# Hybrid decoder trunk: layer 0's scale weights through five buffers of the first stage's own pool

## The chip, the cores and the metric

One Trainium2 chip, of which one core is used. The metric is the device time of one execution in microseconds (us). PE is TensorE, DVE is VectorE, ACT is ScalarE, POOL is GpSimd, and SP is SyncE, whose queue issues every load spoken of here.

## What is computed

Two layers of a decoder trunk over 256 tokens of width 2048, in float32. Each layer has a token-mixing part (four head groups side by side) and a gated feed-forward part, and both are modulated by six vectors that come from one conditioning vector c. Cut to what matters:

```python
def reference(x, c, ada_w, ada_b, norm_mix, ...):
    cond = jax.nn.silu(c)
    for l in range(DEPTH):
        mod = cond @ ada_w[l] + ada_b[l]                  # 2048 x 12288 weights
        sh1, sc1, g1, sh2, sc2, g2 = [m[:, None, :] for m in jnp.split(mod, 6, axis=-1)]
        h = rms_norm(x, norm_mix[l]) * (1.0 + sc1) + sh1  # this stage, in layer 0
        x = x + g1 * hybrid_mixer(h, w_in[l], ...)        # u = h @ w_in comes first
        h = rms_norm(x, norm_ffn[l]) * (1.0 + sc2) + sh2
        x = x + g2 * conv_glu_ffn(h, ffn_up[l], ...)
    return x
```

The change concerns sh1 (shift) and sc1 (scale) of layer 0, which must be there before the first input projection can begin.

## The kernel before

The width of 2048 is cut into 16 chunks of 128 partitions, `k` = 0 to 15. The activations stand transposed (channels on partitions, 256 tokens in the free dimension). The product of c with the adaLN weights is not made on TensorE: `ada_mul` (line 167) lets VectorE multiply a 128x1024 tile of weights, half a chunk's rows, with `cond` and sum along the row. A vector of six needs two such tiles per chunk, 512 KB each. For most of them this runs beside the matmuls of other stages, through `ada_jobs`. For layer 0's shift and scale there is nothing yet to run beside, so they are made in the first stage itself, `mix_in_behind`, one chunk per turn of its loop. This loop is the stage that the change touches. Its turn for chunk `k` is:

1. two loads of scale weights (`ada_load`, L163), and two multiplies on DVE (L167), then `sc` (L470);
2. a load of `wconv`, 512 KB (`load_w`, L242);
3. two loads of shift weights, two multiplies, then `sh` (L470), and `amul` from `sc` (L474);
4. the chunk's normalised activations: `t` on DVE (L394) and `actw` on ACT (L396). A copy is split in two parts for later (ACT L492, DVE L493, tile `act`);
5. matmuls of `wconv` with the chunk (L415, 8 instructions, which the trace shows as 16 passes), a load of `wlq`, 448 KB, and its matmuls (L415, 5 instructions, 10 passes; L427, 2 instructions, 4 passes).

Each turn so loads five tiles of 512 KB and one of 448 KB, all on the one queue of SP, in this order: scale, scale, `wconv`, shift, shift, `wlq`. SP goes through its queue in order: an issue that waits for its buffer holds all that stand behind it. Two rings of buffers decide these waits. All adaLN weights go through the tag `adaw` of the pool `ap_`, three buffers; the loads of weights for TensorE go through the tag `raw` of the pool `weights`, `RAW` = 4 buffers, so that in this stage `wconv` and `wlq` have two each. A load takes a buffer when the last reader of the tile that was in it is done: a multiply on DVE for `adaw`, matmuls for `raw`. Before the loop come the load of x (2 MB), and the norm's sum of squares (`norm_stats`), which shares DVE with the first multiplies. The tiles of the stage lie in its pool `sp`, which is closed at its end.

After the loop come the convolution group's taps on DVE (L621) beside a matrix product of 16 chunks on PE (L322), and then the rest of the layer. The tag `adaw` serves `ada_jobs` from there on.

```python
            for s, m in ((1, sc), (0, sh)):
                if s == 0:
                    w = load_w(io["wconv"][l, k], True)
                ada_dot(l, s, k, raws[s])
```

Of the kernel before, what the change touches and what calls it, by code (L numbers as in the profile page):

```python
# [11 lines left out]
F32 = mybir.dt.float32  # L12
# [8 lines left out]
P = 128  # L21
T = 256
D = 2048
# [43 lines left out]
GATE = ((1, 0, 0, 1, 1), (1, 0, 0, 1, 1))  # L67
DW_LATE = 800
RAW = 4

JOIN = 8
GAINS = 2 * 4 * 64 + 2 * 96 + 2 * 32
# [3 lines left out]
def tile_trunk(ctx: ExitStack, tc: tile.TileContext, io, out, L):  # L76
    nc = tc.nc

    def pool(stack, name, bufs=1, **kw):
        return stack.enter_context(tc.tile_pool(name=name, bufs=bufs, reuse_waits="tile", **kw))  # L80
# [3 lines left out]
    ap_ = pool(ctx, "ada")  # L84
# [16 lines left out]
    def load_constants():  # L101
        nc.sync.dma_start(con, io["con"])
        msk = wp.tile([P, 1024], F32, tag="raw", name="msk", bufs=RAW)[:, 0:2 * P]
        nc.sync.dma_start(msk, io["msk"])
# [37 lines left out]
    def vec(l, name):  # L142
        o, w = VEC[name]
        if o >= NVEC:
            if (l, 1) not in vecs:
                vecs[l, 1] = cp.tile([P, NVECS], F32, name=f"vs{l}")
                nc.sync.dma_start(vecs[l, 1], io["vecs"][l])
            return vecs[l, 1][:, o - NVEC:o - NVEC + w]
        if (l, 0) not in vecs:
            vecs[l, 0] = cp.tile([P, NVEC], F32, tag="vec", name="vec", bufs=1)  # L150
            nc.sync.dma_start(vecs[l, 0], io["vec"][l])
        return vecs[l, 0][:, o:o + w]
# [4 lines left out]

    dots = []

    def ada_load(l, s, j, hf):  # L160
        w = ap_.tile([P, D // 2], F32, tag="adaw", name="adaw", bufs=3)
        with tc.issue_after(last_load[0].ins) if gate[0] else ExitStack():
            nc.sync.dma_start(w, io["ada"][l, s * KD + j, hf])  # L163
        return w

    def ada_mul(w, s, j, hf, raw):
        nc.vector.scalar_tensor_tensor(  # L167
            w, w, 1.0, cond[:, hf * 1024:hf * 1024 + 1024], op0=ALU.mult, op1=ALU.mult,
            accum_out=raw[:, hf, j:j + 1],
        )  # L170

    def ada_dot(l, s, j, raw):
        for hf in range(2):
            ada_mul(ada_load(l, s, j, hf), s, j, hf, raw)

    def run_dots():
        while dots:
# [60 lines left out]
    def load_w(src, whole=False):  # L238

        n = src.shape[-1]  # L240
        raw = wp.tile([P, 1024], F32, tag="raw", name="raw", bufs=RAW)
        last_load[0] = nc.sync.dma_start(raw[:, :n], src)  # L242
        tick(rate[0])
        if whole:
            return raw, None
        hi = wp.tile([P, 1024], F32R, tag="hi", name="hi", bufs=3)
        nc.scalar.copy(hi[:, :n], raw[:, :n])  # L247
        lo = wp.tile([P, 1024], F32R, tag="lo", name="lo", bufs=3)
        sub = nc.vector.tensor_sub(lo[:, :n], raw[:, :n], hi[:, :n].bitcast(F32))  # L249
        if dots:  # L250

            with tc.high_priority(offset=-late[0]), tc.issue_after(sub.ins):
                run_dots()
        return hi, lo
# [79 lines left out]
    def act_whole():  # L334
        return actp.tile([P, 4, T], F32, tag="act", name="actw", bufs=12)
# [12 lines left out]
    def norm_stats(x, sp, pp, tag):  # L348

        ss = pp.tile([P, 2, T], F32, tag=tag, name="ss")  # L350
        acc = sp.tile([P, 4, T], F32, name="nacc")
        for c in range(4):
            xc = x[:, 4 * c:4 * c + 4, :]
            if c == 0:
                nc.scalar.activation(acc, xc, AF.Square)
                continue
            sq = sp.tile([P, 4, T], F32, tag="nsq4", name="sq", bufs=2)
            nc.scalar.activation(sq, xc, AF.Square)
            nc.vector.tensor_add(acc, acc, sq)
        nc.vector.tensor_add(acc[:, 0:2, :], acc[:, 0:2, :], acc[:, 2:4, :])  # L360
        for c in range(2):
            nc.tensor.matmul(ss[:, 0, :], ones, acc[:, c, :], start=(c == 0), stop=(c == 1))
        r = sp.tile([P, T], F32, tag="nr", name="r", bufs=1)
        rsqrt(r, ss[:, 0, :], D)
        return r
# [25 lines left out]
    def norm_chunk(dst, xc, r, a, sh, sp):  # L391

        t1 = sp.tile([P, T], F32, tag="nsq", name="t1", bufs=2)
        nc.vector.scalar_tensor_tensor(t1, xc, a, r, op0=ALU.mult, op1=ALU.mult)  # L394
        if is_whole(dst):
            nc.scalar.activation(dst, t1, AF.Identity, bias=sh)  # L396
            return
        nc.scalar.activation(dst[:, 0, :], t1, AF.Identity, bias=sh)
        nc.vector.scalar_tensor_tensor(  # L399
            dst[:, 1, :], t1, sh, dst[:, 0, :].bitcast(F32), op0=ALU.add, op1=ALU.subtract  # L400
        )

    def norm_hs():
        hs = []
        for _ in range(KD // 2):
            ht = act_pair()
            hs += [ht[:, 0], ht[:, 1]]
        return hs

    def mm_t(ps, w, h, G, first, last):  # L410

        prods = products(w, h, True)
        for m in range(G):
            for i, (ww, xx) in enumerate(prods):
                nc.tensor.matmul(  # L415
                    ps[m // 2][:, m % 2, :], ww[:, m * P:(m + 1) * P], xx,
                    start=(first and i == 0 and m % 2 == 0), stop=(last and i == len(prods) - 1),
                    skip_group_check=True,
                )

    def mm_n(outs, w, h, first, last):

        prods = products(w, h, False)
        for tt in range(2):
            for i, (ww, xx) in enumerate(prods):
                for o, c0, c1, f in outs(tt):
                    nc.tensor.matmul(  # L427
                        o, xx[:, tt * P:(tt + 1) * P], ww[:, c0:c1],
                        start=(first and i == 0 and f), stop=(last and i == len(prods) - 1),
                        skip_group_check=True,  # L430
                    )
# [19 lines left out]
    def mix_in_behind(l, x, sp, pp, mr, conv):  # L451

        r = norm_stats(x, sp, pp, "gp")
        a = cp.tile([P, KD], F32, tag="amul", name="amul", bufs=2)
        g, ab = vec(l, "norm_mix"), vec(l, "ada_b")
        sh = cp.tile([P, KD], F32, name="sh0")
        sc = cp.tile([P, KD], F32, name="sc0")
        raws = [cp.tile([P, 2, KD], F32, name=f"raw0_{i}") for i in range(2)]
        hs, hw = norm_hs(), []
        for _ in range(KD // 4):  # L460
            t = act_whole()
            hw += [t[:, i, :] for i in range(4)]
        ps = [pp.tile([P, 2, T], F32, tag="gp", name="gt") for _ in range(4)]
        px = [pp.tile([P, 2, T], F32, tag="gx", name="gt") for _ in range(4)]
        for k in range(KD):
            for s, m in ((1, sc), (0, sh)):
                if s == 0:
                    w = load_w(io["wconv"][l, k], True)
                ada_dot(l, s, k, raws[s])
                nc.vector.scalar_tensor_tensor(  # L470
                    m[:, k:k + 1], raws[s][:, 0, k:k + 1], ab[:, s * KD + k:s * KD + k + 1],
                    raws[s][:, 1, k:k + 1], op0=ALU.add, op1=ALU.add,
                )
            nc.vector.scalar_tensor_tensor(  # L474
                a[:, k:k + 1], sc[:, k:k + 1], 1.0, g[:, k:k + 1], op0=ALU.add, op1=ALU.mult
            )
            norm_chunk(hw[k], x[:, k, :], r, a[:, k:k + 1], sh[:, k:k + 1], sp)
            split_chunk(hs[k], hw[k])
            mm_t(px, w, hw[k], 8, k == 0, k == KD - 1)
            if k == KD - 1:  # L480
                cv = [mr.tile([P, 4, T], F32, tag=t, name="cv") for t in ("sq4", "acc")]
                cv = [t[:, 2 * i:2 * i + 2, :] for t in cv for i in range(2)]
                for i in range(4):
                    nc.scalar.copy(cv[i], px[i])
                conv(cv)
            w = load_w(io["wlq"][l, k], True)
            mm_t(ps, w, hw[k], 5, k == 0, k == KD - 1)
            mm_n(lambda tt: [(ps[3][:, tt, :], 640, 896, tt == 0)], w, hw[k], k == 0, k == KD - 1)
        return hs, ps, hw

    def split_chunk(dst, src):
        nc.scalar.copy(dst[:, 0, :], src)  # L492
        nc.vector.tensor_sub(dst[:, 1, :], src, dst[:, 0, :].bitcast(F32))  # L493
# [556 lines left out]
    for l in range(L):  # L1050
# [7 lines left out]
        with ExitStack() as s1:  # L1058
            p8 = _Tagged(pool(s1, f"p8_{l}", space=PSUM), {"gp": 4, "gx": 4})
            with ExitStack() as s0:  # L1060
                ug = []

                def conv(q):
                    ug.append(conv_taps(l, conv_glu(l, q, mr), mr))

                sp = pool(s0, f"n1_{l}")
# [289 lines left out]
```

## Time and profile before

| | us |
|---|---|
| median of 3 runs | 2460.51 |
| lowest and highest of these | 2454.77, 2468.78 |
| the profiled execution, device time | 2445.3 |
| its span, from the first to the last instruction | 2443.0 |
| of it, stretch in which `mix_in_behind` turns | about 20 to 155 |

The profiled execution is a run of its own, and some tenths of a per cent faster than the three that were timed. All durations are from it. Busy times and shares are per engine; in the profile a DMA share of 1.00 means that on average all 16 DMA engines of the core had a packet under way. Times in the rows are from the start of the span.

### The profile page before, as it was taken

How to read it: one execution, taken by the hardware profiler on the slowest of the kernel's cores; microseconds unless marked ns; L12 is line 12 of the kernel's file. 1: busy time of each engine (PE TensorE's matmuls, PEld its weight loads, DVE VectorE, ACT ScalarE, POOL GpSimd, SP SyncE). 2: the span in 40 equal slices, each digit the busy share in tenths (PEclk: the TensorE clock that was granted, in tenths of full speed). 3: DMA queues.
4: the chain of work that ended last, by engine and by line, in shares of the span. 5: the costliest groups of instructions: out<-in, count | busy, mean ns of one | idle time of the engine just before them, and what ended most of it. 6: DMA issues, size and time to landing. Idle time of an engine off the chain costs nothing.

```text
span 2443.0 us, 38166 instructions
## 1 busy us (share of the span) xinstructions
PE 2366.8 (97%) x14496; PEld 2095.8 (86%) x14496; DVE 1935.9 (79%) x3212; ACT 1223.7 (50%) x1880; POOL 25.4 (1%) x40
## 2 busy tenths in 40 slices
PE   7889999989999999999999999999999999999999
PEld 5666998978888888888889989998888888888887
DVE  6679988898888887788877999888887765566755
ACT  2124566446555434556344476553655553355543
POOL 0010000000000000000001000000000000000000
PEclk9999999999999999999999999999999999999999
DMA  9975887987777898777875566788767665556554
GB/s 334 342 260 173 280 270 258 350 300 265 239 258 252 293 330 292 242 248 257 306 272 185 180 236 227 271 321 315 236 228 242 220 196 191 190 183 197 189 191 164
DMA packets 169098, 609.82 MB, mean 250 GB/s; under 512 B 19025, under 2 KB 20945, under 8 KB 168401
## 3 DMA queue, kind: packets, MB, share of 16 engines
q1 hardware_dynamic: 168914, 607.39, 72.7%
q8 instruction: 113, 1.85, 0.3%
q14 instruction: 71, 0.58, 0.1%
HBM read 603.12 MB, written 4.19 MB: 249 GB/s over the span
## 4 chain that ended last, share of the span: by engine, by line
PE 84%; DVE 8%; DMA 5%; ACT 2%; issue 1%; SPq 0%; DVEq 0%; ACTq 0%
PE gt L300 39%; PE gt L304 20%; PE gt L279 10%; DMA adaw<-in_ada_dram 5%; PE gt L415 3%; DVE adaw L167 2%; DVE acc L621 2%; PE pv L322 2%; PE pn L322 1%; PE po L591 1%; PE s L565 1%; DVE lo L249 1%; PE pq L322 1%; PE tp L586 1%; PE ss L382 1%
## 5 line engine op out<-in xcount | busy, mean ns | idle before, releaser
L247 ACT CAST hi<-raw 128x1024 fp32r<-128x1024 f32 (+3 forms) x716 | 740.3, 1035 | 854.0 <-PE gt L300 605.5
L249 DVE TENSOR_TENSOR lo<-raw,hi 128x1024 fp32r<-128x1024 f32 (+3 forms) x716 | 858.7, 1202 | 356.8 <-ACT hi L247 354.5
L300 PE MATMUL gt<-act,hi 128*128 128x512 f32 x2816 | 985.0, 396 | 11.7 <-DVE act L399 8.7
L304 PE MATMUL gt<-act,lo 128*128 128x256 f32 x2816 | 785.8, 280 | 2.7 <-DVE lo L249 2.7
L300 PEld LDWEIGHTS gt<-act,hi 128*128 128x128 f32 x2816 | 530.0, 188 | 136.9 <-DVE act L399 9.5
L304 PEld LDWEIGHTS gt<-act,lo 128*128 128x128 f32 x2816 | 532.0, 189 | 4.0 <-DVE lo L249 4.0
L167 DVE SCALAR_TENSOR_TENSOR adaw<-adaw,cond 128x1024 f32<-128x1024 f32 x384 | 465.0, 1219 | 68.8 <-DMA adaw<-in_ada_dram 67.4
L300 PE MATMUL gt<-g,hi 128*128 128x512 f32 x1408 | 490.0, 393 | 0.0
L304 PE MATMUL gt<-g,lo 128*128 128x256 f32 x1408 | 392.9, 279 | 0.2 <-DVE lo L249 0.2
L300 PEld LDWEIGHTS gt<-g,hi 128*128 128x128 f32 x1408 | 263.8, 187 | 60.2
L279 PE MATMUL gt<-act,hi 128*128 128x256 f32 x1600 | 303.3, 287 | 0.0
L304 PEld LDWEIGHTS gt<-g,lo 128*128 128x128 f32 x1408 | 265.2, 188 | 0.7 <-DVE lo L249 0.5
L279 PEld LDWEIGHTS gt<-act,hi 128*128 128x128 f32 x1600 | 251.5, 192 | 1.4 <-DVE x L1121 0.3
L279 PE MATMUL gt<-act,lo 128*128 128x256 f32 x800 | 229.7, 288 | 1.4 <-DVE lo L249 1.4
L279 PEld LDWEIGHTS gt<-act,lo 128*128 128x128 f32 x800 | 153.2, 192 | 2.3 <-DVE lo L249 2.0
L415 PE MATMUL gt<-actw,raw 128*128 128x256 f32 x416 | 103.4, 410 | 25.0 <-ACT actw L396 25.0
L415 PEld LDWEIGHTS gt<-actw,raw 128*128 128x128 f32 x416 | 84.7, 207 | 43.6 <-ACT actw L396 30.8
L1159 ACT ACTIVATE u<-v,vec 128x256 f32<-128x256 f32 x176 | 96.7, 597 | 10.0 <-DVE v L1156 5.2
L621 DVE SCALAR_TENSOR_TENSOR acc<-ug,vec,acc 128x256 f32<-128x256 f32 x240 | 99.3, 475 | 0.0
L1160 DVE SCALAR_TENSOR_TENSOR u<-v,vec,u 128x255 f32<-128x255 f32 x176 | 80.0, 478 | 12.1 <-ACT u L1159 12.1
L1155 ACT COPY v<-gt 128x256 f32<-128x256 f32 x176 | 63.3, 370 | 47.8 <-PE gt L304 34.7
L1163 DVE SCALAR_TENSOR_TENSOR u<-v,vec,u 128x254 f32<-128x254 f32 x176 | 80.1, 479 | 2.6
(290 smaller groups left out, 2146.3 us busy)
## 6 DMA issues: line engine op xcount, KB each, us to landing
adaw<-in_ada_dram SPq DMA_DIRECT2D x384, 512.0 KB, 5.4
raw<-in_wup_dram SPq DMA_DIRECT2D x352, 512.0 KB, 4.3
raw<-in_wdn_dram SPq DMA_DIRECT2D x176, 512.0 KB, 4.4
raw<-in_wo_dram SPq DMA_DIRECT2D x64, 512.0 KB, 5.5
raw<-in_wconv_dram SPq DMA_DIRECT2D x32, 512.0 KB, 4.6
raw<-in_wsqk_dram SPq DMA_DIRECT2D x32, 512.0 KB, 4.5
raw<-in_wlq_dram SPq DMA_DIRECT2D x32, 448.0 KB, 4.6
raw<-in_wnkv_dram SPq DMA_DIRECT2D x32, 412.0 KB, 3.2
```

What stands on the lines that cost most here:

```text
L167: nc.vector.scalar_tensor_tensor(w, w, 1.0, cond[:, hf * 1024:hf * 1024 + 1024], op0=ALU.mult, op1=ALU.mult, accum_out=raw[:, hf, j:j + 1],)
L247: nc.scalar.copy(hi[:, :n], raw[:, :n])
L249: sub = nc.vector.tensor_sub(lo[:, :n], raw[:, :n], hi[:, :n].bitcast(F32))
L279: nc.tensor.matmul(ps[m // 2][:, m % 2, :], ww[:, c], x, start=(k == 0 and i == 0 and m % 2 == 0), stop=(k == K - 1 and i == len(prods) - ...
L300: nc.tensor.matmul(banks[m].rearrange("p a t -> p (a t)"), hi[:, c], x2, start=(k == 0), stop=False, skip_group_check=True,)
L304: nc.tensor.matmul(banks[m][:, 1, :], lo[:, c], acts[k][:, 0, :], start=False, stop=(k == K - 1), skip_group_check=True,)
L322: nc.tensor.matmul(o, x[:, tt * P:(tt + 1) * P], ww[:, kk * N + c0:kk * N + c1], start=(k == 0 and i == 0 and first), stop=(k == K - 1 and ...
L415: nc.tensor.matmul(ps[m // 2][:, m % 2, :], ww[:, m * P:(m + 1) * P], xx, start=(first and i == 0 and m % 2 == 0), stop=(last and i == len ...
L621: nc.vector.scalar_tensor_tensor(acc[:, c, :], ug[:, c, j:j + T], w, acc[:, c, :], op0=ALU.mult, op1=ALU.add)
L1159: nc.scalar.activation(u[:, q, :], v, AF.Identity, scale=w2, bias=fb[:, i:i + 1])
L1160: nc.vector.scalar_tensor_tensor(u[:, q, 1:], v[:, :T - 1], w1, u[:, q, 1:], op0=ALU.mult, op1=ALU.add)
L1163: nc.vector.scalar_tensor_tensor(u[:, q, 2:], v[:, :T - 2], w0, u[:, q, 2:], op0=ALU.mult, op1=ALU.add)
```

## The change

Within `mix_in_behind`, the two loads of scale weights of each chunk take their tiles from the stage's own pool `sp`, under the same tag name but in a ring of `FIRST` = 5 buffers. The two loads of shift weights go on through the three buffers of `ap_`, which the scale's loads no longer use. Nothing else is changed: no instruction is added or removed, and none stands in another place on any engine.

```diff
+FIRST = 5
+
 JOIN = 8
@@
-    def ada_load(l, s, j, hf):
-        w = ap_.tile([P, D // 2], F32, tag="adaw", name="adaw", bufs=3)
+    def ada_load(l, s, j, hf, mp=None):
+        w = (mp or ap_).tile([P, D // 2], F32, tag="adaw", name="adaw", bufs=3 if mp is None else FIRST)
         with tc.issue_after(last_load[0].ins) if gate[0] else ExitStack():
             nc.sync.dma_start(w, io["ada"][l, s * KD + j, hf])
         return w
@@
-    def ada_dot(l, s, j, raw):
+    def ada_dot(l, s, j, raw, mp):
         for hf in range(2):
-            ada_mul(ada_load(l, s, j, hf), s, j, hf, raw)
+            ada_mul(ada_load(l, s, j, hf, mp), s, j, hf, raw)
@@
-                ada_dot(l, s, k, raws[s])
+                ada_dot(l, s, k, raws[s], sp if s else None)
```

What moves is not the place of an instruction but what it waits for. On SP's queue, at the start of the stage, before the change (chunk 0 and chunk 1; `DVE_49` is DVE's counter, on which an issue waits for a multiply; the `DMAHW` counters make every DMA wait for the landing of the eighth DMA ahead of it; `PE_49` is PE's):

```order
L163 DMA adaw_166<-in_ada_dram 128x1024
L163 DMA adaw_169<-in_ada_dram 128x1024
L242 DMA raw_173<-in_wconv_dram 128x1024 [waits DMAHW0_49]
L163 DMA adaw_175<-in_ada_dram 128x1024 [waits DMAHW1_49]
L163 DMA adaw_178<-in_ada_dram 128x1024 [waits DMAHW2_49,DVE_49]
L242 DMA raw_196<-in_wlq_dram 128x896 [waits DMAHW3_49]
L163 DMA adaw_205<-in_ada_dram 128x1024 [waits DMAHW4_49,DVE_49]
L163 DMA adaw_208<-in_ada_dram 128x1024 [waits DMAHW5_49,DVE_49]
L242 DMA raw_212<-in_wconv_dram 128x1024 [waits DMAHW6_49]
L163 DMA adaw_214<-in_ada_dram 128x1024 [waits DMAHW7_49,DVE_49]
```

The same place on SP's queue with the change:

```order
L165 DMA adaw_166<-in_ada_dram 128x1024
L165 DMA adaw_169<-in_ada_dram 128x1024
L244 DMA raw_173<-in_wconv_dram 128x1024 [waits DMAHW0_49]
L165 DMA adaw_175<-in_ada_dram 128x1024 [waits DMAHW1_49]
L165 DMA adaw_178<-in_ada_dram 128x1024 [waits DMAHW2_49]
L244 DMA raw_196<-in_wlq_dram 128x896 [waits DMAHW3_49]
L165 DMA adaw_205<-in_ada_dram 128x1024 [waits DMAHW4_49]
L165 DMA adaw_208<-in_ada_dram 128x1024 [waits DMAHW5_49]
L244 DMA raw_212<-in_wconv_dram 128x1024 [waits DMAHW6_49]
L165 DMA adaw_214<-in_ada_dram 128x1024 [waits DMAHW7_49]
```

Before, the fourth adaLN load is the first that waits for a multiply. Now none of the seven shown does.

In the middle of the stage (SP's queue, the turn of chunk 4), before the change every adaLN load waits for DVE:

```order
L163 DMA adaw_322<-in_ada_dram 128x1024 [waits DMAHW6_49,DVE_49]
L163 DMA adaw_325<-in_ada_dram 128x1024 [waits DMAHW7_49,DVE_49]
L242 DMA raw_329<-in_wconv_dram 128x1024 [waits DMAHW0_49,PE_49]
L163 DMA adaw_331<-in_ada_dram 128x1024 [waits DMAHW1_49,DVE_49]
L163 DMA adaw_334<-in_ada_dram 128x1024 [waits DMAHW2_49,DVE_49]
L242 DMA raw_352<-in_wlq_dram 128x896 [waits DMAHW3_49,PE_49]
```

And with the change:

```order
L165 DMA adaw_322<-in_ada_dram 128x1024 [waits DMAHW6_49]
L165 DMA adaw_325<-in_ada_dram 128x1024 [waits DMAHW7_49]
L244 DMA raw_329<-in_wconv_dram 128x1024 [waits DMAHW0_49,PE_49]
L165 DMA adaw_331<-in_ada_dram 128x1024 [waits DMAHW1_49,DVE_49]
L165 DMA adaw_334<-in_ada_dram 128x1024 [waits DMAHW2_49,DVE_49]
L244 DMA raw_352<-in_wlq_dram 128x896 [waits DMAHW3_49,PE_49]
```

The scale's loads have lost their wait for DVE. They still need a multiply to be done, five scale loads back, but the shift's loads ahead of them on the queue have by then waited for a later one.

## Rows read from the trace of the kernel before

**Rows 1.** The page: span, and the chain that ended last, by engine

```profile
span 2443.0 us, 38166 instructions
...
PE 84%; DVE 8%; DMA 5%; ACT 2%; issue 1%; SPq 0%; DVEq 0%; ACTq 0%
```

**Rows 2.** The chain in 25 to 150 us, by line, shares of that stretch

```profile
by line: DMA adaw<-in_ada_dram 63.1%; DVE adaw L167 26.0%; ACT actw L396 4.1%; DVE act L493 3.4%; ACT act L492 3.3%; DVE sh L470 1.8%; issue 1.2%
```

**Rows 3.** Waits, 25 to 150 us: engine, line, releaser, total, times, longest

```profile
PE gt L415 <- ACT actw L396: 21.5, 10, 3.4
DVE adaw L167 <- DMA adaw<-in_ada_dram: 20.6, 29, 2.0
DVE act L493 <- ACT act L492: 14.2, 14, 1.0
```

**Rows 4.** Waits of SP's queue, 25 to 150 us, same columns

```profile
SPq L163 <- DVE adaw L167: 63.5, 28, 3.4
SPq L163 <- DVE sh L470: 19.2, 14, 2.6
SPq L163 <- DVE sc L470: 10.2, 11, 1.8
...
SPq L242 <- PE gt L415: 0.9, 2, 0.6
```

**Rows 5.** Timeline: chunk 1's sc, chunk 3's turn, chunk 15's sc (start, duration, us)

```profile
23.51 0.22 DVE L470 SCALAR_TENSOR_TENSOR sc<-raw,vs 128x1 f32<-128x1 f32 x1
...
38.03 5.88 PE L415 MATMUL gt<-actw,raw 128*128 128x256 f32 x26 [1.91 <-ACT actw L396]
...
38.79 1.22 DVE L167 SCALAR_TENSOR_TENSOR adaw<-adaw,cond 128x1024 f32<-128x1024 f32 x1
...
43.75 1.03 PE L427 MATMUL gt<-raw,actw 128*128 128x256 f32 x4
...
45.06 1.22 DVE L167 SCALAR_TENSOR_TENSOR adaw<-adaw,cond 128x1024 f32<-128x1024 f32 x1 [1.70 <-DMA adaw<-in_ada_dram]
...
46.33 0.22 DVE L470 SCALAR_TENSOR_TENSOR sh<-raw,vs 128x1 f32<-128x1 f32 x1
...
46.59 0.51 ACT L396 ACTIVATE actw<-t,sh 128x256 f32<-128x256 f32 x1 [8.17 <-DVE sh L470]
...
47.15 7.57 PE L415 MATMUL gt<-actw,raw 128*128 128x256 f32 x26 [2.37 <-ACT actw L396]
...
149.36 0.22 DVE L470 SCALAR_TENSOR_TENSOR sc<-raw,vs 128x1 f32<-128x1 f32 x1
```

**Rows 6.** Stretches: length, busy per engine (count), granted clock, DMA share, GB/s

```profile
5.00:15.00 10.00, 4.71 (x6) 1.33 (x4) 4.43 (x5) 8.63 (x10) 0.00 (x0) 1.00 1.02 403
25.00:150.00 125.00, 103.50 (x430) 86.04 (x429) 87.84 (x182) 12.77 (x28) 0.00 (x0) 0.93 0.95 342
...
20.00:40.00 20.00, 16.65 (x69) 14.16 (x70) 14.63 (x31) 3.07 (x7) 0.00 (x0) 1.00 1.00 363
100.00:125.00 25.00, 21.66 (x90) 17.98 (x90) 17.64 (x36) 2.35 (x6) 0.00 (x0) 0.93 0.94 332
470.00:480.00 10.00, 10.00 (x86) 10.00 (x85) 8.32 (x10) 3.15 (x3) 0.00 (x0) 1.00 1.01 407
180.00:190.00 10.00, 10.00 (x31) 5.48 (x30) 10.00 (x27) 0.00 (x0) 0.00 (x0) 1.00 0.44 140
```

**Rows 7.** DMA issues, 25 to 150 us: count, KB each, median us to landing

```profile
adaw<-in_ada_dram SPq DMA_DIRECT2D x55, 512.0 KB, 5.2
raw<-in_wconv_dram SPq DMA_DIRECT2D x14, 512.0 KB, 5.8
raw<-in_wlq_dram SPq DMA_DIRECT2D x14, 448.0 KB, 5.7
```

**Rows 8.** Loads of `adaw`, 25 to 150 us: issue to landing

```profile
DMA to landing us min/median/max: 3.7/5.2/7.2
```

## Prediction

> **What bounds the kernel now.** The page first: the chain that ended last is PE for 84% of the span, with DMA at 5% [rows 1]. So the kernel is TensorE's, but not everywhere, and the change acts on one stretch only. The chain of that stretch, 25 to 150 us, is the second view: 63% of it lies between issue and landing of an adaLN load, 26% in the multiplies that read them, and PE is not in it [rows 2]. The waits say the same from the engines' side. PE waits 21.5 us for `actw`, which needs `sh`, which needs the multiplies. DVE, which makes them, waits 20.6 us for loads to land [rows 3]. And SP's queue, which issues the loads, waits for DVE to give buffers back, 93 us in three rows, but hardly for PE [rows 4]. It is a circle: load, multiply, free buffer, next load. A load takes 5.2 us to land [rows 7, 8] and only three can be on the way, so the circle turns no faster than its latency lets it.
>
> The period of a turn comes from two rows of the timeline. `sc` of chunk 1 starts at 23.51 and that of chunk 15 at 149.36 [rows 5]: 125.85 us for 14 turns, **8.99 us a turn**. A turn loads 5 x 512 KB + 448 KB = 3008 KB = 3.08 MB. At the 342 GB/s of 25 to 150 us [rows 6] that is 9.01 us, which agrees. The DMA share is 0.95 all that while. The loads are therefore close to busy already, and the question is how much faster they go when more are queued.
>
> **What the change does, part by part.** No work is added or removed. What goes is DVE's wait in the issue of the scale's loads. By the rings, the shift load before a scale load pair of chunk k+1 has waited for the first shift multiply of chunk k-1, and the scale loads behind it need only multiplies that are older. So up to seven adaLN tiles are landed or on the way ahead of DVE instead of three.
>
> Three floors bound the new turn.
>
> DVE: in 14 turns it waits 20.6 us for landings [rows 3], 1.47 us a turn. Without them a turn is 8.99 - 1.47 = **7.52 us**. This still has the 14.2 us that DVE waits for ACT at `act` in each turn [rows 3], 1.0 us a turn, which the change leaves alone. No gain in the loads can bring more than these 20.6 us, plus 0.8 us at most in chunk 15.
>
> PE: the passes of a turn take 5.88 + 1.03 = **6.91 us** [rows 5], at a granted clock of 1.00 (2.4 GHz). The clock's mean over the stage is 0.93 [rows 6], so it stands at 1.2 GHz for about 14% of it, and 0.07 x 125 = 8.8 us of passes are lost. A turn hit by this had 7.57 + 1.03 = 8.60 us of passes, 1.7 more [rows 5], so some five are hit. The one shown came after 2.37 us of idle PE, and such gaps should get rarer. If five were hit as now, and each held the next turn up by 8.6 - 8.0 us, that is 3 us. I take nothing for it and leave the 3 us in the range.
>
> DMA: at the rate of a well filled queue. The rows give three. At the start of the program, where the loads of x and the first adaLN loads go out one after the other without a wait for DVE, 403 GB/s for 10 us. In 470 to 480 us, with PE fully busy, 407. The best longer stretch of this stage, 20 to 40 us at a share of 1.00, gives 363 [rows 6]. 3.08 MB are then 7.64, 7.57 and 8.49 us. I take the middle, (405 + 363)/2 = 384 GB/s, since in the stage there are always loads enough now but the two high rates come from stretches of 10 us alone: **8.02 us a turn**. It is above both other floors, so the stage stays with DMA.
>
> Does SP really get ahead? The ring of `raw` is unchanged, and a weight load that waits on PE holds the shift loads behind it. `actw` of chunk 3 ends at 46.59 + 0.51, 8.3 us after the first multiply at 38.79, of which 1.7 us was a wait for a landing [rows 5]: 6.6 us without. The `wconv` passes are 16 of 26, 16/26 x 5.88 = 3.6 us, so `wconv`'s buffer is free 10.2 us after a turn begins. At 8 us a turn, SP issues the `wconv` of chunk k some 2.2 us into the turn of k-1, and the second shift load by about 4.6 us into it, when the first shift multiply of k-1 is done. They are needed 3.4 and 4.6 us into the turn of k (the second multiply of the shift could have begun at 45.06 - 1.70, 4.6 us after 38.79, and the first a multiply before it [rows 5]), 8 us after they were issued, against a landing time of 5.2 us and at most 7.2 [rows 8]. This holds, with 1 to 3 us to spare. The scale loads go out some 10 us ahead. So the wait moves from DVE's multiplies to PE's release of `raw`, where it costs nothing.
>
> What is gained: 14 turns x (8.99 - 8.02) = **13.6 us**. Chunks 0 and 1 give nothing I count, because there DVE is busy with the norm's sums and first multiplies. After the stage PE and DVE are both fully busy (10.00 of 10 us each in 180 to 190) with DMA at 0.44 [rows 6], so they are what sets the pace, and everything there starts earlier by as much as the stage ends earlier. The tiles that are laid later over the new buffers wait at most for scale multiplies, which come before the last `t` on DVE; I cost that at nothing, and any wait there could be no longer than a multiply, 1.22 us [rows 5].
>
> The profiled execution took 2445.3 us, its span 2443.0 [rows 1], so 2.3 us lie around it. 2445.3 - 13.6 = 2431.7, a ratio of 0.9944. The median of the three runs is 2460.51, and the same ratio gives **2447 us**.
>
> **A rule that speaks against it.** Rows 6 show 403 and 407 GB/s from one core, for 10 us at a time. The Trainium skill, page "DMA: Bandwidth & Descriptors", section "Where 436 GB/s comes from", says that for transfers between HBM and SBUF a limit of about 358 GB/s per core is the one that binds. By it a turn is an estimated 8.60 us, the gain 5.4 us and the time 2455 us. The trace does not agree for bursts; for a whole stage no row here decides it, and the rival below is this case.
>
> **The rivals.**
>
> The DMA engines were the limit already. For it: a share of 0.95, and no longer stretch of the stage above 363 GB/s. Against it: 403 and 407 elsewhere, and DVE's 29 waits, the longest 2.0 us [rows 3], which lie behind loads that were issued late. At 363 a turn is 8.49 us, the gain 14 x 0.5 = 7.0 us: 2453.5 us.
>
> The wait moves to `raw`. If the passes of chunk k-2 end more than some 3 us later than reckoned above, `wconv` holds the shift loads as long as DVE did, and DVE waits again, for the shift instead of the scale. For it: PE has 6.91 us of passes in a turn of 8. Against it: SP's queue waits 0.9 us for the conv matmuls now [rows 4]. Gain 0 to 3 us: 2459 us.
>
> Slower: more transfers in flight get in each other's way, and the rate falls. For it: 25 us of the stage went at 332 GB/s with a share of 0.94 [rows 6], so full engines do not always mean full speed. It decides below 342 GB/s. At 332 a turn is 9.28 us, and the time 4 us longer, 2464.5 us; at 313 GB/s it is 9.85 us a turn and 12 us longer, 2472.5 us. Against it: where more is queued, in 5 to 15 us, the rate is the highest.
>
> **How the numbers follow.** About 0.5% of this kernel's time, 12.3 us, is what a measurement can tell from no change. Forecast, gain 9 to 20 us: 0.58, its own range 2441 to 2452. Engines at their limit, gain 3 to 9: 0.27. `raw` holds, gain 0 to 3: 0.10. Slower: 0.05. Of the forecast's 0.58, 0.46 lie above 12.3 us, so faster by over 0.5% is 0.46. Slower by over 0.5% is the lower part of the last case, 0.03. The rest, 0.51, is within 0.5%. The range reaches from DVE's floor of 7.52 us (a gain of 21 us and a little scatter) to a gain of nearly nothing: 2438 to 2459.
>
> **What would show it.** In the profile after: turns of about 8.0 us between the `sc` of chunk 1 and of chunk 15, a rate of 380 to 390 GB/s with a share of 1.0, DVE's wait for `adaw` landings down from 20.6 to about 7 us, and SP's waits moved to L242 behind PE. If DVE's wait goes and the turn stays over 8.5, the DMA floor was wrong. If SP waits at L242 and DVE's wait stays, it was the ring. If the stage gets shorter and the whole does not, something after it gave the time back, and the claim on PE and DVE there was wrong.

## The result

The changed kernel takes 2433.38 us (median of 13 executions, 2420.03 to 2450.05) against 2456.64 us for the kernel before (13 executions, 2446.18 to 2478.77). The medians lie 23.3 us apart. The measured ratio of the executions is 0.9889, with a 95% interval of 0.9866 to 0.9912: 27 us faster, 22 to 33 by the interval. The forecast was 2447 us, a gain of 13.6, and a range down to 2438. The direction and the circle that it named were right; the gain came out about twice as large, or 1.7 times by the medians.

The page of the changed kernel, lines that answer to [rows 1]:

```profile
span 2430.6 us, 38134 instructions
PE 85%; DVE 6%; DMA 6%; ACT 2%; issue 1%; SPq 0%; DVEq 0%; ACTq 0%
```

All line numbers of the changed kernel are two higher: L169 is the multiply (L167 before), L165 the adaLN load, L244 the weight load, L472 `sc` and `sh`, L417 and L429 the matmuls.

The timeline gives `sc` of chunk 1 and of chunk 15, as at the two ends of [rows 5]:

```profile
23.53 0.22 DVE L472 SCALAR_TENSOR_TENSOR sc<-raw,vs 128x1 f32<-128x1 f32 x1
```

```profile
131.01 0.22 DVE L472 SCALAR_TENSOR_TENSOR sc<-raw,vs 128x1 f32<-128x1 f32 x1
```

That is 107.48 us for 14 turns, **7.68 us a turn** instead of 8.99. The turns into chunks 3 and 4 are still longer (8.7 and 8.3 us); the later ones are 7.5 to 7.8, and the ten from chunk 5 (`sc` at 55.37) to chunk 15 take 7.56 us on average.

One of those later turns in the timeline of the changed kernel (start, duration, us):

```profile
63.44 0.33 SPq L244 DMA_DIRECT2D raw<-in_wconv_dram  x1
...
63.89 1.55 SPq L165 DMA_DIRECT2D adaw<-in_ada_dram  x2
...
66.44 0.22 DVE L472 SCALAR_TENSOR_TENSOR sh<-raw,vs 128x1 f32<-128x1 f32 x1
...
67.67 0.43 DVE L495 TENSOR_TENSOR act<-actw,act 128x256 fp32r<-128x256 f32 x1 [1.01 <-ACT act L494]
68.02 1.22 DVE L169 SCALAR_TENSOR_TENSOR adaw<-adaw,cond 128x1024 f32<-128x1024 f32 x1
...
69.16 1.22 DVE L169 SCALAR_TENSOR_TENSOR adaw<-adaw,cond 128x1024 f32<-128x1024 f32 x1
...
70.42 0.22 DVE L472 SCALAR_TENSOR_TENSOR sc<-raw,vs 128x1 f32<-128x1 f32 x1
```

The multiplies shown follow one another with no wait for a landing, where [rows 5] had one of 1.70 us. The only wait of DVE that the rows show is the 1.01 us for ACT at `act`.

Stretches of the changed kernel, columns as in [rows 6]: length, busy of PE, PE's loads, DVE, ACT and POOL, granted clock, DMA share, GB/s.

```profile
25.00:131.00 106.00, 95.88 (x428) 80.44 (x427) 86.15 (x179) 12.78 (x28) 0.00 (x0) 1.00 1.00 396
15.00:20.00 5.00, 2.05 (x4) 1.18 (x4) 4.75 (x11) 0.53 (x2) 0.00 (x0) 1.00 1.03 411
20.00:40.00 20.00, 18.53 (x75) 15.92 (x76) 15.88 (x35) 3.09 (x7) 0.00 (x0) 1.00 0.89 343
100.00:125.00 25.00, 22.31 (x102) 18.67 (x101) 20.76 (x45) 2.74 (x6) 0.00 (x0) 1.00 1.03 408
```

The loads ran at 396 GB/s over the stage and at 408 in its later part, where [rows 6] had 342 and 332. At 15 to 20 us, where DVE is still busy with the norm, they run on at 411. In 20 to 40 us the share falls to 0.89: there lies the longest of SP's waits for PE at a weight load (the 7.4 us below, until 27.6), and the two long turns, from 30.8 to 47.8 us, follow it. The granted clock is 1.00 where it was 0.93.

Waits of the changed kernel in 25 to 131 us, by engine (answers to [rows 3]), then of SP's queue (answers to [rows 4]); columns: total us, times, longest.

```profile
DVE act L495 <- ACT act L494: 14.2, 14, 1.0
PE gt L417 <- ACT actw L398: 10.1, 12, 1.2
DVE adaw L169 <- DMA adaw<-in_ada_dram: 2.4, 3, 1.3
```

```profile
SPq L244 <- PE gt L417: 46.0, 14, 7.4
SPq L244 <- PE gt L429: 14.2, 14, 1.7
SPq L165 <- DVE adaw L169: 9.4, 12, 1.2
```

DVE's wait for landings went from 20.6 us to 2.4. SP's wait for DVE's buffers, 93 us before, is 9.4 now, and 60.2 us of waiting for PE at the weight loads stands in its place. Almost all of what DVE still waits for landings comes behind the longest of these. First DVE's wait in 30 to 45 us, then SP's in 20 to 45:

```profile
DVE adaw L169 <- DMA adaw<-in_ada_dram: 2.1, 2, 1.3
```

```profile
SPq L244 <- PE gt L417: 11.3, 3, 7.4
```

The shift loads of chunk 2 stand on the queue behind a `wconv` that PE held until 27.6 us, and landed late. The two long turns are together 1.9 us above the later ones.

### The profile page after: what moved, and what is told of

Same layout as the page of the kernel before. It is cut to its first block, busy times and chain, and to the rows that moved or that the text cites. A ratio compares the mean times of both kernels' runs of the same rounds, so it can differ in the third digit from the quotient of the medians.

```text
span 2430.6 us, 38134 instructions
## 1 busy us (share of the span) xinstructions
PE 2366.6 (97%) x14496; PEld 2096.9 (86%) x14496; DVE 1935.5 (80%) x3212; ACT 1224.5 (50%) x1880; POOL 24.5 (1%) x40
## 4 chain that ended last, share of the span: by engine, by line
PE 85%; DVE 6%; DMA 6%; ACT 2%; issue 1%; SPq 0%; DVEq 0%; ACTq 0%
PE gt L302 40%; PE gt L306 20%; PE gt L281 8%; PE gt L417 4%; DMA adaw<-in_ada_dram 4%; DVE acc L623 2%; PE pn L324 1%; PE pv L324 1%; DVE adaw L169 1%; DVE lo L251 1%; PE po L593 1%; PE s L567 1%; PE pq L324 1%; ACT hi L249 1%; PE tp L588 1%
## 5 line engine op out<-in xcount | busy, mean ns | idle before, releaser
L169 DVE SCALAR_TENSOR_TENSOR adaw<-adaw,cond 128x1024 f32<-128x1024 f32 x384 | 463.7, 1218 | 34.5 <-DMA adaw<-in_ada_dram 31.8
L417 PE MATMUL gt<-actw,raw 128*128 128x256 f32 x416 | 96.3, 389 | 12.9 <-ACT actw L398 12.9
L417 PEld LDWEIGHTS gt<-actw,raw 128*128 128x128 f32 x416 | 79.6, 194 | 29.6 <-ACT actw L398 18.9
```

The lines of the kernel that those rows point to most:

```text
L169: nc.vector.scalar_tensor_tensor(w, w, 1.0, cond[:, hf * 1024:hf * 1024 + 1024], op0=ALU.mult, op1=ALU.mult, accum_out=raw[:, hf, j:j + 1],)
L417: nc.tensor.matmul(ps[m // 2][:, m % 2, :], ww[:, m * P:(m + 1) * P], xx, start=(first and i == 0 and m % 2 == 0), stop=(last and i == len ...
```

## The experiments

The first question was what holds the turn at 7.5 us now, the second what the change consists of (five buffers, two rings, or another place in memory), the third where the rest of the difference is. "Turn" below is the time from `sc` of chunk 1 to `sc` of chunk 15, divided by 14, as above. `sc` of chunk 1 starts at 23.5 to 23.7 us; in `ring2` it starts at 25.61, and in the three kernels that leave work out (`mul_less`, `load_less`, `both_less`) at 22.82, 22.61 and 21.58.

| run | buffers for adaLN | sc of chunk 15 at, us | turn, us | span after that sc, us |
|---|---|---|---|---|
| before | one ring of 3 | 149.36 | 8.99 | 2293.6 |
| b_again | one ring of 3 | 154.64 | 9.36 | 2287.0 |
| b_again2 | one ring of 3 | 153.19 | 9.25 | 2303.9 |
| ring3 | one ring of 3, stage's pool | 148.10 | 8.90 | 2303.3 |
| ring2 | one ring of 2, stage's pool | 180.34 | 11.05 | 2291.9 |
| ring4 | one ring of 4, stage's pool | 130.38 | 7.63 | 2289.0 |
| ring4_timed | the same | 130.70 | 7.66 | 2288.8 |
| ring5 | one ring of 5, stage's pool | 130.22 | 7.61 | 2285.0 |
| the change | rings of 5 and 3 | 131.01 | 7.68 | 2299.6 |
| a_again | rings of 5 and 3 | 131.25 | 7.69 | 2316.5 |
| mul_less | rings of 5 and 3 | 129.85 | 7.64 | 2304.6 |
| load_less | rings of 5 and 3 | 128.69 | 7.58 | 2301.9 |
| both_less | rings of 5 and 3 | 120.88 | 7.09 | 2302.3 |

The rows of `sc` of chunk 15 behind the table, in the order `ring3`, `ring4`, `ring5`, `ring2`:

```profile
148.10 0.22 DVE L472 SCALAR_TENSOR_TENSOR sc<-raw,vs 128x1 f32<-128x1 f32 x1
```

```profile
130.38 0.22 DVE L472 SCALAR_TENSOR_TENSOR sc<-raw,vs 128x1 f32<-128x1 f32 x1
```

```profile
130.22 0.22 DVE L472 SCALAR_TENSOR_TENSOR sc<-raw,vs 128x1 f32<-128x1 f32 x1
```

```profile
180.34 0.22 DVE L472 SCALAR_TENSOR_TENSOR sc<-raw,vs 128x1 f32<-128x1 f32 x1
```

### The pool, or the number of buffers

`ring3`, `ring5`, `ring4` and `ring2` put scale and shift together through one ring in the stage's pool, of as many buffers as the name says:

```diff
-FIRST = 5
+FIRST = 3
@@
-                ada_dot(l, s, k, raws[s], sp if s else None)
+                ada_dot(l, s, k, raws[s], sp)
```

> Layer 0's scale and shift weights go through one ring of three buffers in the stage's own pool: the place in memory is that of the change, the number of tiles ahead of VectorE is that of the kernel before. If the number of tiles ahead is what counts: turns of about 9.0 us between the sc of chunk 1 and of chunk 15 (8.99 before), VectorE waits 15 to 25 us for adaLN landings in the stage, about 345 GB/s, time ratio to before 1.00. If the pool or the addresses count: turns of about 7.5 us as in the changed kernel, ratio 0.99.

Measured: turns of 8.90 us and a ratio to before of 1.0002 (0.9955 to 1.0048). The place in memory gives no gain that these numbers can show.

> Scale and shift together through one ring of five buffers in the stage's own pool: five tiles ahead instead of three (before) and seven or eight (the change). If the rate of the loads grows with what is queued: turns between 7.6 and 8.3 us, 370 to 405 GB/s, ratio 0.990 to 0.996. If two separate rings are needed because the shift's loads hold the scale's: turns of 8.7 us or more.

Measured: turns of 7.61 us at 399 GB/s, ratio 0.9874 (0.9808 to 0.9941), a little better than the 0.990 to 0.996 that were expected. One ring of five does what the two rings of the change do, and the shift's loads don't hold the scale's.

> Scale and shift together through one ring of four buffers in the stage's own pool. If the gain comes with each tile that is ahead until the loads are always queued: turns of 7.9 to 8.4 us, between the 8.90 of three buffers and the 7.61 of five. If one more tile is all that was missing: 7.6 us, as with five.

Measured: turns of 7.63 us. One more buffer than before is all that was missing in the stage; the expectation that the gain comes bit by bit fell.

> One ring of four buffers for scale and shift, timed. If one buffer more than before takes the whole gain: stage's end at 134 to 136 us and a ratio to before of 0.986 to 0.992, like the change. If the five and three of the change bring more in other executions: a ratio above 0.993.

Measured: ratio 0.9882 (0.9847 to 0.9917), `sc` of chunk 15 at 130.70. Four buffers take the whole gain.

The stretch 25 to 130 us, with three, four and five buffers in this order (columns as above):

```profile
25.00:130.00 105.00, 87.46 (x370) 73.32 (x369) 74.78 (x155) 10.95 (x24) 0.00 (x0) 0.95 0.95 348
```

```profile
25.00:130.00 105.00, 95.09 (x426) 79.85 (x426) 85.88 (x178) 12.78 (x28) 0.00 (x0) 1.00 1.01 401
```

```profile
25.00:130.00 105.00, 94.87 (x427) 79.69 (x426) 85.96 (x178) 12.77 (x28) 0.00 (x0) 1.00 1.01 399
```

The DMA issues of the same stretches, again three, four, five buffers (count, KB each, median us to landing):

```profile
adaw<-in_ada_dram SPq DMA_DIRECT2D x48, 512.0 KB, 5.1
```

```profile
adaw<-in_ada_dram SPq DMA_DIRECT2D x54, 512.0 KB, 6.2
```

```profile
adaw<-in_ada_dram SPq DMA_DIRECT2D x54, 512.0 KB, 7.5
```

From four buffers to five the rate stays at 400 GB/s, and the landing time grows by 1.3 us: nothing is gained by having the fifth tile under way.

This is what a circle does. A buffer is taken until its tile has landed and been multiplied (1.22 us), and a turn needs four buffers' worth. The landing time of the profile counts from the start of the issue, so the 0.33 us of the issue are in it already. With three buffers and the median landing time of before, 5.2 us, a turn is 4/3 x (5.2 + 1.22) = 8.6 us; measured were 8.99. With four it would be 4/4 x 6.42 = 6.4 us if the landing time stayed, which is under the floors of 7.4 to 7.6 found below. It did not stay: it rose to 6.2, and the turn stopped at 7.6. `ring2` asks the same of a smaller ring:

> Scale and shift through one ring of two buffers. If the circle of load, multiply and free buffer sets the turn: four loads through two buffers, 4/2 x (0.33 us issue + landing + 1.22 us multiply). With the landing time of before, 5.2 us, that is 13.5 us a turn; with the shortest landing seen before, 3.7 us, 10.5. So 10.5 to 13.5 us, 230 to 290 GB/s. If the rate of the DMA engines were the limit with three buffers already: about 9 us a turn as with three.

Measured: turns of 11.05 us at 284 GB/s, with a landing time of 4.0 us:

```profile
25.00:130.00 105.00, 75.08 (x294) 61.34 (x293) 61.75 (x127) 8.89 (x20) 0.00 (x0) 0.89 0.83 284
```

```profile
adaw<-in_ada_dram SPq DMA_DIRECT2D x39, 512.0 KB, 4.0
```

4/2 x (4.0 + 1.22) = 10.4 us. The expectation counted the issue's 0.33 us a second time; with them the sum is 11.1, and its agreement with 11.05 is luck. Counted once, the sum is about 5% short at two buffers as at three: it leaves out the short waits of a landed tile for DVE, and takes the median landing, which here lies under the mean. And it needs the landing time of the kernel itself, 4.0 us here; with the 5.2 of before, `ring2` would have been put at 12.8. So the circle is shown by the way the turn goes with the number of buffers (11.05, 8.90, 7.63), and the formula tells a turn beforehand only as well as the landing time is known.

### What holds the turn now

`mul_less` leaves out the second scale multiply of each turn:

```diff
         for hf in range(2):
-            ada_mul(ada_load(l, s, j, hf, mp), s, j, hf, raw)
+            w = ada_load(l, s, j, hf, mp)
+            if s == 1 and hf == 1:
+                nc.vector.tensor_copy(raw[:, hf, j:j + 1], w[:, 0:1])
+                continue
+            ada_mul(w, s, j, hf, raw)
```

> The changed kernel with the second scale multiply of each turn left out (its tile is still loaded; one 128x1 copy stands for the multiply), so VectorE has about 1.2 us less in a turn: its floor is about 6.4 us, that of the loads is 3.08 MB at 408 GB/s, 7.55 us. If the loads are a floor of their own at 7.55: turns of 7.4 to 7.6 us. If only VectorE's 7.52 us holds the changed kernel: turns of 6.9 to 7.1 us, where PE's passes (6.91 us) come next.

Measured: turns of 7.64 us. Its waits and its stretch, 25 to 130 us:

```profile
DVE adaw L169 <- DMA adaw<-in_ada_dram: 17.7, 15, 2.0
```

```profile
25.00:130.00 105.00, 94.48 (x421) 79.23 (x421) 70.44 (x164) 12.78 (x28) 0.00 (x0) 1.00 1.00 398
```

The 14 x 1.22 = 17.1 us that DVE was spared came back as 17.7 us of waiting for landings: the loads are a floor of their own, at 398 GB/s. From chunk 5 to chunk 15 the turns are 7.55 us, which is 3.08 MB at 408 GB/s.

The chain of the changed kernel in 25 to 131 us says the same. As in [rows 2], most of it lies between issue and landing of an adaLN load:

```profile
by line: DMA adaw<-in_ada_dram 64.3%; PE gt L417 23.8%; DVE adaw L169 8.3%; PE gt L429 1.6%; ACT actw L398 1.5%; SPq L244 1.2%; issue 0.9%; DVE sh L472 0.7%; SPq L165 0.1%
```

`load_less` leaves out the second scale load and multiplies the first tile twice:

```diff
         for hf in range(2):
-            ada_mul(ada_load(l, s, j, hf, mp), s, j, hf, raw)
+            if s == 1 and hf == 1:
+                w2 = w
+            else:
+                w2 = ada_load(l, s, j, hf, mp)
+            w = w2
+            ada_mul(w, s, j, hf, raw)
```

> The changed kernel with the second scale load of each turn left out (the multiply reads the first tile a second time), 2.56 MB a turn: at 408 GB/s 6.3 us. If VectorE's 7.52 us is a floor of its own: turns of 7.45 to 7.55 us, with a DMA share of 0.85 or so. If only the loads hold the changed kernel: turns of 6.9 to 7.1 us, by PE's passes.

Measured: turns of 7.58 us, just above the range given, and the DMA engines no longer full (0.92, where about 0.85 was expected):

```profile
25.00:130.00 105.00, 97.46 (x435) 81.83 (x434) 85.48 (x181) 12.77 (x28) 0.00 (x0) 1.00 0.92 339
```

The average of 7.58 looks like the 7.52 us that the prediction had worked out for DVE, but this is luck. It holds one turn of 10.4 us, behind the wait for PE at the start of the stage, in which DVE's waits for landings lie:

```profile
DVE adaw L169 <- DMA adaw<-in_ada_dram: 2.8, 2, 2.4
```

From chunk 4 on each of the eleven turns takes 7.36 us, with no such wait in any of them:

```profile
47.72 0.22 DVE L477 SCALAR_TENSOR_TENSOR sc<-raw,vs 128x1 f32<-128x1 f32 x1
```

```profile
128.69 0.22 DVE L477 SCALAR_TENSOR_TENSOR sc<-raw,vs 128x1 f32<-128x1 f32 x1
```

So DVE is a floor of its own, at 7.36 us, and in the changed kernel the loads lie above it.

`both_less` is `load_less` with the copy of `mul_less` in place of the second multiply:

```diff
             w = w2
+            if s == 1 and hf == 1:
+                nc.vector.tensor_copy(raw[:, hf, j:j + 1], w[:, 0:1])
+                continue
             ada_mul(w, s, j, hf, raw)
```

> The changed kernel with the second scale load and its multiply of each turn left out (one 128x1 copy of the first tile stands for them): 2.56 MB a turn, 6.3 us at 408 GB/s, and VectorE's floor 6.4 us. With both floors lowered PE is next: its passes are 6.91 us. Turns of 6.9 to 7.1 us if the two floors found are all that held the changed kernel at 7.5; 7.4 us or more if a third one, unnamed, holds it as well.

Measured: turns of 7.09 us, and PE takes over:

```profile
25.00:130.00 105.00, 101.32 (x461) 87.20 (x460) 73.78 (x173) 16.25 (x35) 0.00 (x0) 1.00 0.94 356
```

PE is busy for 101.3 of 105 us (the last few of these belong to the next stage), and the turns from chunk 4 to chunk 15 take 6.89 us. So three floors lie within 0.7 us of each other: PE at 6.9, DVE at 7.36 and the loads at 3.08 MB / 408 GB/s = 7.55. Less work for DVE alone brings nothing here, and fewer loads alone bring 0.2 us a turn.

### The rest of the difference

`b_again` and `b_again2` are the kernel before, `a_again` is the changed one, with no edit, for more profiles.

> The kernel before, profiled once more. If the stage is as steady as its work, it ends (actw of chunk 15) at 154 us give or take 1, as in the first profile (154.3), and the rest of the span is 2280 to 2300 us; then the stage explains about 19 us of the measured difference and the rest must be scatter. If the first profile was a lucky one for the stage: it ends at 158 us or later, and the whole of 27 us lies in the stage.

> The kernel before, profiled a third time: as for the second, 154 us give or take 1 if the stage is steady, 158 us or later if it is not.

Measured: `sc` of chunk 15 at 154.64 and 153.19, `actw` of chunk 15 done at 159.9 and 159.1 (154.3 in the first profile). The rows of `sc`, `b_again` first:

```profile
154.64 0.22 DVE L470 SCALAR_TENSOR_TENSOR sc<-raw,vs 128x1 f32<-128x1 f32 x1
```

```profile
153.19 0.22 DVE L470 SCALAR_TENSOR_TENSOR sc<-raw,vs 128x1 f32<-128x1 f32 x1
```

With three buffers the stage is not the same in every trace: four have turns of 8.90 to 9.36 us, and the one that the prediction read was among the shorter. Whether the execution or the chip makes the difference is not shown. `b_again` and `b_again2` ran on another chip than `ring3`, and there the kernel before was slower as a whole (median 2466.97 us, against 2455.42 beside `ring3`), while the changed one was not (2433.12, against 2433.38 in the first comparison).

> The changed kernel once more, with its own comparison to the kernel before. If the stage alone makes the difference: it ends at 135 us give or take 1, and the ratio is 0.990 to 0.994 (19 to 20 us of 2456 is 0.992). If something after the stage gains too, in every execution: the ratio comes out at 0.987 to 0.990 again, and the rest of the span is some 6 us shorter than in the two profiles of before.

Measured: ratio 0.9862 (0.9824 to 0.9900), `actw` of chunk 15 done at 135.5, and a rest that is the longest of all. So neither case came out: the ratio is beyond that of the stage alone, but the rest is not shorter. The five traces with four or more buffers and all the work have `sc` of chunk 15 between 130.22 and 131.25. The three of the kernel before have it at 152.40 on average, the two of the change at 131.13: the stage gives **21.3 us** (20.2 if `ring3` is counted with the kernel before).

The span after that `sc` is the same work in every run of the table, and takes 2285 to 2317 us. Kernels with three buffers lie between 2287 and 2304, with more between 2285 and 2317, so there is no sign of a gain or loss by the number of buffers there. The five traces with rings of 5 and 3 (2300 to 2317) do lie above the three with one ring of four or five (2285 to 2289), but whole executions don't bear a difference out: the median of `ring4_timed` is 2436.38 us, those of the change 2433.38 and 2433.12. One cause of the spread is seen in the matmuls of layer 0's feed-forward part, where the kernel before, 580 to 880 us, and the changed one, 562 to 864 us, run nearly the same passes (PE line, form, count, busy us, mean ns):

```profile
L300 PE MATMUL gt<-act,hi 128*128 128x512 f32 x667 | 231.3, 391 | 0.0
```

```profile
L302 PE MATMUL gt<-act,hi 128*128 128x512 f32 x664 | 234.7, 399 | 0.0
```

In the first pair of profiles, the changed kernel leads by 22 us at 450 us and by 12.4 at the end. Some 6 to 7 of these 10 us are its passes in this part, about 860 of them at 399 ns and not 391. In `ring3`, which is the kernel before in all but the place of its buffers, they are long as well, and it ended 8 us behind the profile of before. So the change is not needed for the long passes. In the second layer the same kernel has both: 391 ns in the first trace of the change, 399 in `a_again`. In the first layer both traces of the change have 399 ns and the three of the kernel before 391 to 394, so there it is not settled whether the execution or the kernel decides. A single pair of profiles would have put the gain at 12.4 us, which happens to be near the forecast, for a wrong reason.

The stage's 21.3 us lie just below the measured 22 to 33, and 2 us under the difference of the medians. The second comparison of the change, at 0.9862, lies further out. The three traces of the kernel before (2443.9 to 2459.4 us) are shorter executions than most of those timed, so the stage as it is in its longer executions was not seen. Whether chance in the slow passes makes up the few us between, or the stage of before is longer on average than in its three traces, is not settled.

## Why the prediction was wrong

**The bound was read rightly.** The chain through the adaLN loads was the circle that the change opened. DVE's wait for landings went from 20.6 us to 2.4, below the 7 that were forecast.

**DVE's floor was nearly right.** 7.52 us by subtraction, 7.36 in the turns of `load_less` that wait for no landing. The subtraction was 0.16 too high, and this moved nothing, since the loads lie above both.

**The step that failed is the DMA floor.** The prediction took 384 GB/s and 8.02 us, half way between the bursts (403 and 407) and the stage's best 20 us (363). Measured were 396 over the stage, with turns of 7.68 us, and 408 in its later part, 7.55 us. The bursts were the right rows. The 363 was no property of the DMA engines, since that stretch ran in the same circle of three buffers that the change removes: a rate that is limited by a wait was used as evidence on what comes when the wait goes. The share of 0.95 misled as well. It read like 5% of room, but with it went 360 GB/s for a share of 1.00 (342 / 0.95), and in the changed kernel the same share is worth 396. With a turn of 7.55 us in place of 8.02, the working of the prediction gives 14 x 1.44 = 20.2 us, and 2440 us; with the 7.68 of the whole stage, 18.3 us and 2442.

**The second step is the turn of before.** 8.99 us came from one execution; the other two traces of the same kernel have 9.36 and 9.25. With the mean of the three, 9.20, and the measured 7.68, 14 turns give 21.3 us.

**What the miss adds up to.** The forecast is 13.6 us above the measured median. Of these, 14 x (8.02 - 7.68) = 4.8 us are the loads, 14 x (9.20 - 8.99) = 2.9 us the turn of before, and 3.9 us the level from which the prediction started: 2460.51 us from three executions, where 13 gave 2456.64. The last 2 us stay open.

**The circle was not worked out.** The prediction named it, and with the rows it had, 4/3 x (5.2 + 1.22) = 8.6 and 4/4 of the same = 6.4 would have said that a single buffer more may put the stage on its floors.

**Of the rivals.** That the engines were at their limit already fell: 396 GB/s over 106 us. The Trainium skill, page "DMA: Bandwidth & Descriptors", section "Where 436 GB/s comes from", has about 358 GB/s as the limit that binds between HBM and SBUF; here, with one core at work, the trace does not agree for a whole stage either. That the wait moves to `raw` came true as to SP's queue (60.2 us at L244). It cost about 2 us, in the two long turns at the start of the stage, and hardly anything after them, where DVE waits for one landing, 0.4 us, in 55 to 125 us. Landing took longer than allowed for, 7.8 us at the median in place of 5.2, without making DVE wait, as the scale's loads and most of the shift's were issued early enough. That more transfers in flight lower the rate fell; the rate rose.

**The clock.** The 3 us left for it were not needed. The granted clock is 1.00 in the whole stretch (0.93 before), and PE's longest wait for `actw` in it is 1.2 us (3.4 before).

**After the stage.** The gain reaches the end of the program on average, as the comparisons of whole executions show, though single profiles hide it under a spread of 30 us.

## What to carry to other kernels

Where a ring of buffers feeds a consumer, work out the circle first: buffers needed per turn over buffers there, times landing (counted from the issue) plus use. If that lies above every engine's own time per turn, add buffers until the turn stops falling, and no more; here four in one ring did what eight in two did. The landing time is no constant in this: it was 4.0, 5.1, 6.2 and 7.5 us with two, three, four and five buffers. An average over turns can hide a start-up turn, as it did in `load_less`: read the floor from turns that repeat. And take the rate of full queues from a stretch in which nothing waited for buffers, not from the stretch that is to be sped up.

The Trainium skill, page "Perfetto Trace Analysis", section "Optimization Strategy", says that a gap which repeats on the engine that should be saturated can mean too few buffers. The trace agrees: 29 waits of DVE before, three after.

## What the hardware showed

A DMA share near 1 does not mean that the rate is near its highest. At a share of 0.95 the stage moved 342 GB/s and at 1.00 it moved 396, 16% more for 5% more share; `load_less`, with its engines idle now and then, has 339 at 0.92. Of the stage's packets of 512 B and more, 4.5% took over 300 ns in the kernel before, 0.4% in the changed one, and 3.9% in `load_less`, where the usual packet of 4 KB takes 159 ns. In these three traces the slow packets go with the lower rates, and not with the fuller queue. Why they are slow no run here shows.

Matmuls of 512 columns at a granted clock of 1.00 had a mean of 391 ns in one execution and 399 ns in another for some 300 us on end, and the same kernel has both in its second layer. No run here shows why.
